# Where the two parts of a split weight lie in SBUF, modulo 256 bytes, in a float32 decoder block on one core

## Chip, core and metric

One NeuronCore of one Trainium2 chip runs the whole program. The metric is the device time of one execution in microseconds (us). The kernel before took 2196.67 us, the median of three runs (2195.61 to 2196.71).

## What is computed

The reference is one layer of a decoder block in float32, on 512 tokens of width 2048:

- RMSNorm, then one input projection. Its columns feed two token mixers: eight heads of dilated sliding-window attention, and eight heads of sparse attention with a compressed, a selected and a window branch mixed by sigmoid gates.
- RMSNorm of each mixer's output, one output projection of width 2048, the residual.
- RMSNorm, then a SwiGLU feed-forward of hidden width 5632: `h + (silu(hn @ w_gate) * (hn @ w_up)) @ w_down`.
- A last RMSNorm.

```
proj = rmsnorm(x) @ w_in
h = x + concat(rmsnorm(o_a), rmsnorm(o_b)) @ w_out
h = h + (silu(hn2 @ w_gate) * (hn2 @ w_up)) @ w_down
```

## The kernel before

**Three products for one.** Every large operand is split in two parts of type float32r: `wh` holds the weight rounded, `wl` the remainder. The activations lie split in the same way in two long-lived tiles `ah` and `al`, and in the feed-forward also in `B11h`/`B11l`, `T1h`/`T1l` and so on. One product is three matmuls into the same bank: `wh` with `ah`, `wh` with `al`, `wl` with `ah` (`mm3`, lines 162 to 165; `mm`, lines 1002 to 1005, is the same without a group check). A 128x128 piece of `wh` or `wl` is the stationary operand, which a weight load (PEld) brings into TensorE; the rows of the activations are the moving operand, 512 or 256 columns long.

**Halves.** Weights come from memory in units of 1024 columns (tile `raw`, four buffers) and, for the down projection, of 512 (`rawd`, two buffers). A `Job` (line 121) turns one half of 512 columns into `wh` (line 134, ScalarE copies and rounds) and `wl` (line 137, VectorE subtracts). `jobs` lists all halves in the order in which TensorE takes them; `next_half` (line 170) hands out one and keeps three or four splits ahead. One half is four stationary pieces, so it feeds 12 matmuls.

**Stages in order.** First the columns for the compressed branch (tiles `pc`), then keys, values and queries with the attention steps woven in (`pp`, and `phid` where the compression weights, units `w1`, are the *moving* operand against the stationary `kvs`), then the output projection (`pab`). These halves come from the loop at line 144; all but `w1` feed matmuls of 512 moving columns. Then 44 blocks `f` of the feed-forward's hidden rows. A block is seven products P1 to P7 of 256 moving columns (a Strassen-Winograd scheme over 2x2 quarters, here "quads"), two halves each, so 168 matmuls; `quad_jobs` (line 743) builds its 14 jobs. In every fourth block from `f` = 4 on, the 16 halves of the down projection for the four blocks before stand between the products (`dn_job`, line 794, and `down`, line 1053; 512 moving columns; banks `pd` and the bank of P3, which the profile groups under the name `P`). The last 16 halves of the down projection go through `kept` (line 797) into room of the activation tiles and are used by `last` (256 columns, `pl`).

**Places.** `placed` (line 82) takes a tile that is 64 elements longer than needed and hands out a slice that begins `at` elements into it. `wsplit` (line 117) chooses `at`: `MH = ML = 32` elements where the job has `even` set, `WH = WL = 16` elements otherwise. The activation tiles use `MH` and `ML`. In the built program all these tiles begin 128 bytes past a multiple of 256, so the activations' rows begin at 0 modulo 256 bytes, weight parts with `even` at 0 too, and weight parts without it at 192, that is 64 bytes below. Each stationary piece is 512 bytes long in a partition and each activation row 2048 or 1024, so every piece of a half keeps its half's place modulo 256. In the kernel before, `even` is set in the first half of P1 of every block (line 788) and nowhere else. Counted in the built program: 4800 matmuls of 512 columns have their `wh` or `wl` at 192; of those of 256 columns in the quads 6864 have it at 192 and 528 at 0.

One other stationary operand has several places: the gate weights `wgs` (lines 266 and 312 to 314) take 192 bytes for each of the 16 steps `k`, so that `k` = 0, 1, 2, 3 lie at 128, 64, 0 and 192 modulo 256, and so on. They are the weights of 512-column matmuls of 48 and of 24 stationary columns.

Of the kernel before, what the change touches and what calls it, by code (L numbers as in the profile page):

```python
# [71 lines left out]
def block_kernel(ctx: ExitStack, tc: tile.TileContext, xt, wst, wdn, smalls, wg, w2c, bias, ident_in, out):  # L72
# [29 lines left out]
    def load_to(n):  # L102
        while state["dma"] < min(n, len(units)):
            u = state["dma"]
            t = wp.tile([128, 1024], F32, tag="raw", name="raw", bufs=LA)
            for k in range(2 if u < TWO else 1):
                c = slice(512 * k, 512 * k + 512) if u < TWO else slice(0, 1024)
                sp.dma_start(t[:, c], wst[u][:, c])
            raws[u] = t
            state["dma"] += 1  # L110

    late = {}
    jobs = []
# [27 lines left out]
    def half_of(u, k):  # L141
        return lambda: raws[u][:, 512 * k:512 * k + 512]

    for u, d in enumerate(units):
        if d[0] != "quad":
            for k in range(2):
                jobs.append(Job(half_of(u, k), load=lambda u=u: load_to(u + 1)))

    n_plain = len(jobs)
    total = n_plain + 14 * FB + KB * NPH  # L150
# [95 lines left out]
    def tokens(*accs):  # L246
        return [[a[:, 128 * t:128 * t + 128] for a in accs] for t in range(accs[0].shape[-1] // 128)]
# [176 lines left out]
    def evac(p, tag, scale=None, keep=False):  # L424

        t = tmp()
        if scale is None:
            dve.tensor_tensor(t, p, r1, op=OP.mult)
        else:
            dve.scalar_tensor_tensor(t, p, scale, r1, op0=OP.mult, op1=OP.mult)  # L430
        ph, pl = (MH, ML) if tag[0] == "k" else (WH, WL)
        h = placed(kvq(tag), S, ph, tag=tag + "h", name=tag + "h")
        l = placed(kvq(tag), S, pl, tag=tag + "l", name=tag + "l")
        act.activation(h, t, AF.Copy)
        dve.tensor_tensor(l, t, h.bitcast(F32), op=OP.subtract)
        return (h, l, t) if keep else (h, l)
# [212 lines left out]
    def proj_block(upto=None):  # L649
        return ps.tile([128, 512], F32, tag="proj", name="pp", bufs=2)  # L650
# [40 lines left out]
    for j in range(NH):  # L691
# [5 lines left out]
        p = proj_block()  # L697
# [8 lines left out]
        p = proj_block()  # L706
# [3 lines left out]
        p = proj_block()  # L710
        for half in range(2):
            in_unit(p, half)
        k = evac(p, "ka")
        v = V()
        queue.append(Att("dil", q, k, v, ba, None, {}, True, True, head_done(j, 0)))
        p = proj_block()
# [10 lines left out]
    dn = {}  # L727
# [9 lines left out]
    def load_fin(n):  # L737
        while len(fin) < min(n, KB // 2):
            k = 2 * len(fin)
            fin.append(wp.tile([128, 1024], F32, tag="raw", name="fin", bufs=LA))  # L740
            sp.dma_start(fin[-1].rearrange("p (n c) -> p n c", n=2), wdn[NPH - 1, k:k + 2].rearrange("n p c -> p n c"))

    def quad_jobs(f, order):

        u = base_u + 4 * f

        def q(i, k):
            return raws[u + i][:, 512 * k:512 * k + 512]

        def comb(o, a, b, op):  # L750
            return lambda: dve.tensor_tensor(o(), a(), b(), op=op)  # L751

        def nxt(i):
            return lambda: load_to(u + 4 + i + 1)

        r = {}
        for k in range(2):
            A11, A21, A22, A12 = (lambda i=i, k=k: q(i, k) for i in range(4))
            if f == 0:
                def s1(A11=A11, A21=A21, A22=A22):  # L760
                    comb(A11, A11, A21, OP.subtract)()
                    comb(A21, A21, A22, OP.add)()

                r["P1", k] = Job(A11, load=nxt(-1))
                r["P5", k] = Job(A21, prep=s1)
                r["P7", k] = Job(A11)
                r["P4", k] = Job(A22)
            else:
                r["P1", k] = Job(A11)
                r["P7", k] = Job(A11, prep=comb(A11, A11, A21, OP.subtract))  # L770
                r["P4", k] = Job(A22, post=comb(A21, A21, A22, OP.add))
                r["P5", k] = Job(A21)
            r["P6", k] = Job(A22, prep=comb(A22, A22, A11, OP.subtract))
            r["P2", k] = Job(A12)
            r["P3", k] = Job(A12, prep=comb(A12, A12, A22, OP.subtract))
        if f + 1 < FB:
            if f == 0:
                r["P6", 1].post = nxt(1)
                r["P3", 1].post = nxt(3)
            else:  # L780
                r["P6", 1].post = nxt(0)
                r["P5", 1].post = nxt(1)
                r["P3", 1].post = nxt(3)
        else:
            r["P6", 1].post = lambda: load_fin(1)
            r["P5", 1].post = lambda: load_fin(2)
            r["P3", 1].post = lambda: load_fin(LA)
        r["P1", 0].even = True
        return [r[p, k] for p in order for k in range(2)]

    ORDER0 = ("P1", "P5", "P2", "P7", "P4", "P6", "P3")
    ORDER = ("P1", "P7", "P4", "P6", "P5", "P2", "P3")

    def dn_job(p, nb):
        return Job(lambda: dn[p, nb], post=load_dn)

    def kept(nb):
        def f():
# [5 lines left out]
    for f in range(FB):  # L804
        qj = quad_jobs(f, ORDER if f else ORDER0)
        p = f // PH - 1
        nb = 0
        for i, name in enumerate(ORDER if f else ORDER0):
            sched.append(("q", f, name))
            jobs += qj[2 * i:2 * i + 2]  # L810
            if f and f % PH == 0 and i:
                for _ in range(3 if i < 5 else 4):
                    if nb < KB:
                        sched.append(("d", p, nb))
                        jobs.append(dn_job(p, nb))
                        nb += 1
    for nb in range(KB):
        jobs.append(Job(lambda nb=nb: fin[nb // 2][:, 512 * (nb % 2):512 * (nb % 2) + 512], dst=kept(nb),
                        post=(lambda nb=nb: load_fin(nb // 2 + LA + 1)) if nb % 2 else None))
# [3 lines left out]
    def out_unit(half, tag="proj"):  # L823
        p = ps.tile([128, 512], F32, tag=tag, name="pab", bufs=2)
        c = 8 - 8 * half
        run_unit([(p, ah[:, c + k, :], al[:, c + k, :], k == 0, k == 7) for k in range(8)])
        return p
# [54 lines left out]
    for nb in range(KB):  # L882
        while "hs" not in rest and (nb == 4 and not idle() or nb == 2 and (queue or cur["s"])):
            step()
        p = out_unit(1, ("proj", "sc", "t")[nb // 2 % 3])
# [86 lines left out]
    for i in range(KB):  # L972
        nb = PASS2[i]
        p = out_unit(0)
# [96 lines left out]
    for kind, a, b in sched:  # L1071
# [3 lines left out]
        f, name = a, b  # L1075
        product(f, name)
        if f == 0:
            if name == "P7":
                r = st["rs2"] = Rsqrt(tokens(sacc), D, rab.v[:, :4])
# [154 lines left out]
```

## Time and profile before

| what | value |
|---|---|
| median of three runs | 2196.67 us |
| the profiled execution's own time | 2196.02 us |
| its span, first to last instruction | 2194.3 us |
| PE busy | 2172.3 us, 13856 matmuls |
| PEld busy | 1951.7 us |
| DVE busy, ACT busy | 1571.1 us, 969.3 us |
| granted TensorE clock, mean | 0.997 |
| HBM read | 223.94 MB |

PE is TensorE's matmul side, PEld its weight loads, DVE is VectorE, ACT ScalarE. "Mean ns of one" of a matmul reaches from its start to the end of its pipeline, and matmuls overlap, so the mean is longer than the distance from one start to the next. That distance, here called the **step**, is read from the start times in the timeline. Times in the timeline count from the span's start.

### The profile page before, as it was taken

Reading aid. Unit: us, or ns where it says so; the run is one execution under the profiler, and the core shown is the slowest. Engines: PE = TensorE matmul, PEld = TensorE weight load, DVE = VectorE, ACT = ScalarE, POOL = GpSimd, SP = SyncE. Lnnn points to the kernel's source line nnn. Section 1 sums busy time; section 2 is a strip of 40 time slices with the busy share of each in tenths; the row PEclk is TensorE's granted clock in tenths of the full one; section 3 lists DMA queues with packets and bytes.
Section 4 is the critical chain, followed back from the end, with each engine's and each line's share of the span. In section 5 each row is a group of like instructions: output and inputs, shape, how many; then the busy total and the mean of one; then the engine's idle time right before and its main releaser. Section 6 shows DMA issues by size and latency. Waiting matters only on the chain.

```text
span 2194.3 us, 35893 instructions
## 1 busy us (share of the span) xinstructions
PE 2172.3 (99%) x13856; PEld 1951.7 (89%) x13856; DVE 1571.1 (72%) x3051; ACT 969.3 (44%) x1861; POOL 39.5 (2%) x46
## 2 busy tenths in 40 slices
PE   9999999999999999999999999999999999999997
PEld 7788888888887888989899999989898999999897
DVE  6755656356667588979687777869596877778686
ACT  6544444344444255535343443435353434434356
POOL 0000000000000000000000000000000000000003
PEclk9999999999999999999999999999999999999999
DMA  6442222322224232333333333333333333333233
GB/s 222 144 137 80 80 80 75 101 79 80 89 75 156 96 96 68 116 115 92 107 111 107 95 113 105 104 95 120 112 97 106 106 111 93 115 106 102 84 124 106
DMA packets 82252, 230.47 MB, mean 105 GB/s; under 512 B 8736, under 2 KB 13216, under 8 KB 82080
## 3 DMA queue, kind: packets, MB, share of 16 engines
q1 hardware_dynamic: 82080, 228.17, 33.3%
q8 instruction: 109, 1.79, 0.3%
q14 instruction: 63, 0.52, 0.1%
HBM read 223.94 MB, written 4.19 MB: 104 GB/s over the span
## 4 chain that ended last, share of the span: by engine, by line
PE 96%; DVE 2%; ACT 1%; issue 0%; DMA 0%; SPq 0%; DVEq 0%; ACTq 0%
PE P L1003 13%; PE P L1005 13%; PE P L1004 13%; PE pp L163 6%; PE pp L165 6%; PE pp L164 6%; PE pd L165 4%; PE pd L164 4%; PE pd L163 4%; PE P L165 3%; PE P L164 3%; PE P L163 3%; PE pab L163 3%; PE pab L165 3%; PE pab L164 3%; PE pt L512 1%
## 5 line engine op out<-in xcount | busy, mean ns | idle before, releaser
L134 ACT ACTIVATE wh<-raw 128x512 fp32r<-128x512 f32 x888 | 548.1, 628 | 524.3 <-PE P L1004 175.3
L137 DVE TENSOR_TENSOR wl<-raw,wh 128x512 fp32r<-128x512 f32 x888 | 596.2, 685 | 65.6 <-ACT wh L134 58.3
L1005 PE MATMUL P<-ah,wl 128*128 128x256 f32 x1056 | 292.3, 277 | 0.2 <-DVE wl L137 0.2
L1003 PE MATMUL P<-ah,wh 128*128 128x256 f32 x1056 | 292.2, 277 | 0.0
L1004 PE MATMUL P<-al,wh 128*128 128x256 f32 x1056 | 292.1, 277 | 0.0
L163 PE MATMUL pp<-ah,wh 128*128 128x512 f32 x640 | 259.1, 405 | 0.0
L165 PE MATMUL pp<-ah,wl 128*128 128x512 f32 x640 | 251.5, 393 | 0.0
L164 PE MATMUL pp<-al,wh 128*128 128x512 f32 x640 | 250.4, 391 | 0.0
L751 DVE TENSOR_TENSOR raw<-raw 128x512 f32<-128x512 f32 x352 | 241.3, 686 | 3.4
L134 ACT ACTIVATE wh<-rawd 128x512 fp32r<-128x512 f32 x160 | 101.1, 632 | 280.6 <-PE pd L164 162.6
L1003 PEld LDWEIGHTS P<-ah,wh 128*128 128x128 f32 x1056 | 199.0, 188 | 0.8
L1004 PEld LDWEIGHTS P<-al,wh 128*128 128x128 f32 x1056 | 198.8, 188 | 0.9
L1005 PEld LDWEIGHTS P<-ah,wl 128*128 128x128 f32 x1056 | 198.8, 188 | 0.5 <-DVE wl L137 0.5
L1067 DVE TENSOR_TENSOR hs<-hs,pd 128x512 f32<-128x512 f32 x98 | 67.3, 687 | 132.5 <-PE pd L165 132.4
L165 PE MATMUL pd<-ah,wl 128*128 128x512 f32 x392 | 154.4, 394 | 0.0
L164 PE MATMUL pd<-al,wh 128*128 128x512 f32 x392 | 153.7, 392 | 0.0
L163 PE MATMUL pd<-ah,wh 128*128 128x512 f32 x392 | 152.1, 388 | 0.0
L165 PEld LDWEIGHTS pp<-ah,wl 128*128 128x128 f32 x640 | 120.2, 188 | 26.4
L164 PEld LDWEIGHTS pp<-al,wh 128*128 128x128 f32 x640 | 120.6, 188 | 19.9
L163 PEld LDWEIGHTS pp<-ah,wh 128*128 128x128 f32 x640 | 120.6, 188 | 19.6
L137 DVE TENSOR_TENSOR wl<-rawd,wh 128x512 fp32r<-128x512 f32 x160 | 109.6, 685 | 22.8 <-ACT wh L134 22.1
L501 ACT ACTIVATE e<-e,st 128x512 f32<-128x512 f32 (+1 forms) x96 | 54.1, 563 | 133.7 <-DVE st L499 133.7
(277 smaller groups left out, 4924.4 us busy)
## 6 DMA issues: line engine op xcount, KB each, us to landing
raw<-in_wst_dram SPq DMA_DIRECT2D x311, 512.0 KB, 3.5
rawd<-in_wdn_dram SPq DMA_DIRECT2D x160, 256.0 KB, 2.6
bias<-in_bias_dram SPq DMA_DIRECT2D x16, 320.0 KB, 2.9
xc<-in_xt_dram SPq DMA_DIRECT2D x16, 256.0 KB, 2.8
hs<-in_xt_dram SPq DMA_DIRECT2D x16, 256.0 KB, 5.3
fin<-in_wdn_dram SPq DMA_DIRECT2D x8, 512.0 KB, 3.7
out_dram<-hs SPq DMA_DIRECT2D x10, 256.0 KB, 2.2
out_dram<-hs SPq DMA_DIRECT2D x3, 512.0 KB, 3.4
```

Of the source, the lines that this page charges most:

```text
L134: act.activation(self.h, self.src(), AF.Copy)
L137: dve.tensor_tensor(self.l, self.src(), self.h.bitcast(F32), op=OP.subtract)
L163: pe.matmul(o, wh, mh, start=start, stop=False)
L164: pe.matmul(o, wh, ml, start=False, stop=False)
L165: pe.matmul(o, wl, mh, start=False, stop=stop)
L501: act.activation(et, et, AF.Exp, bias=m, scale=-1.0, accum_out=den)
L512: pe.transpose(p[:, 128 * (o + b):128 * (o + b) + 128], self.e[t][:, 128 * b:128 * b + 128], ident)
L751: return lambda: dve.tensor_tensor(o(), a(), b(), op=op)
L1003: pe.matmul(o, wh, mh, start=start, stop=False, skip_group_check=True)
L1004: pe.matmul(o, wh, ml, start=False, stop=False, skip_group_check=True)
L1005: pe.matmul(o, wl, mh, start=False, stop=stop, skip_group_check=True)
L1067: dve.tensor_tensor(hs[:, nb, :], hs[:, nb, :], p, op=OP.add)
```

## The change

Three lines of one file. The jobs of all units but the quads get `even`, so do the jobs of the down projection but the last 16, and the first half of P1 keeps it in blocks 0 and 1 alone.

```diff
     for u, d in enumerate(units):
         if d[0] != "quad":
             for k in range(2):
-                jobs.append(Job(half_of(u, k), load=lambda u=u: load_to(u + 1)))
+                jobs.append(Job(half_of(u, k), load=lambda u=u: load_to(u + 1), even=True))
...
-        r["P1", 0].even = True
+        r["P1", 0].even = f < 2
...
     def dn_job(p, nb):
-        return Job(lambda: dn[p, nb], post=load_dn)
+        return Job(lambda: dn[p, nb], post=load_dn, even=True)
```

The instructions, their order on every engine, their sizes and their waits are the same in both programs; addresses differ. Counted in the built program after: the 4800 matmuls of 512 columns have their weight part at 0 modulo 256, the place of the moving rows; 7368 of the quads' matmuls have it at 192 and 24 at 0. In the 128 matmuls of `phid` the moving operand is a weight part, and goes from 192 to 0 against a stationary operand at 128.

## Prediction

> **What bounds the kernel now.** I read the engines' shares first, then the chain that ended last, then the costliest groups.
>
> ```profile
> span 2194.3 us, 35893 instructions
> PE 2172.3 (99%) x13856; PEld 1951.7 (89%) x13856; DVE 1571.1 (72%) x3051; ACT 969.3 (44%) x1861; POOL 39.5 (2%) x46
> PEclk9999999999999999999999999999999999999999
> ...
> PE 96%; DVE 2%; ACT 1%; issue 0%; DMA 0%; SPq 0%; DVEq 0%; ACTq 0%
> ...
> L1005 PE MATMUL P<-ah,wl 128*128 128x256 f32 x1056 | 292.3, 277 | 0.2 <-DVE wl L137 0.2
> L1003 PE MATMUL P<-ah,wh 128*128 128x256 f32 x1056 | 292.2, 277 | 0.0
> ...
> L163 PE MATMUL pp<-ah,wh 128*128 128x512 f32 x640 | 259.1, 405 | 0.0
> ...
> L163 PEld LDWEIGHTS pp<-ah,wh 128*128 128x128 f32 x640 | 120.6, 188 | 19.6
> ```
>
> TensorE is busy 99% of the span at an undiminished clock, and 96% of the chain is matmuls. The groups wait for almost nothing: their last column is 0.0 to 0.2 us. So a change of a matmul's step goes one for one into the time, in both directions: 2194.3 - 2172.3 = 22 us of PE idle time is all that a slower PE could eat into, and it lies where the change hardly reaches (the start, the norm between the two feed-forward parts, the end). ScalarE and VectorE do the same splits as before to other addresses; with 44% and 72% they have room, and a slower PE only gives them more. No DMA, wait or queue moves, so the whole question is what one matmul's step costs when its weight load reads from another place.
>
> **The steps, read from the timeline.** First a run of 36 matmuls of 512 columns in the down projection, weights at 192 modulo 256:
>
> ```profile
> 935.94 0.39 PE L163 MATMUL P<-ah,wh 128*128 128x512 f32 x1
> ...
> 944.18 0.28 PE L1003 MATMUL P<-T4h,wh 128*128 128x256 f32 x1
> ```
>
> (944.18 - 935.94) / 36 = 228.9 ns per step. The means of the same kind in the grouped view show that it isn't the same for the three matmuls of a product:
>
> ```profile
> L165 PE MATMUL pd<-ah,wl 128*128 128x512 f32 x392 | 154.4, 394 | 0.0
> L164 PE MATMUL pd<-al,wh 128*128 128x512 f32 x392 | 153.7, 392 | 0.0
> L163 PE MATMUL pd<-ah,wh 128*128 128x512 f32 x392 | 152.1, 388 | 0.0
> ```
>
> Their mean, 391.3 ns, is 162.4 ns over the step, which is the pipeline behind it; so 388, 392 and 394 are steps of 225.6, 229.6 and 231.6 ns. Now the only place where the trace has weights at the moving rows' own place over a long run: the first half of P1 (12 matmuls of 256 columns, at 0), followed by its second half (12 at 192).
>
> ```profile
> 930.42 0.28 PE L1003 MATMUL P<-B11h,wh 128*128 128x256 f32 x1
> ...
> 931.86 0.28 PE L1003 MATMUL P<-B11h,wh 128*128 128x256 f32 x1
> ...
> 933.22 0.28 PE L1003 MATMUL P<-ah,wh 128*128 128x256 f32 x1
> ```
>
> At 0: 1.44 / 12 = 120.0 ns. At 192: 1.36 / 12 = 113.3 ns. Same operands, same sizes, same engine work beside it: the equal place costs 6.7 ns a matmul at 256 columns.
>
> **The change part by part.**
>
> *Part 1, P1's first half from block 2 on.* 42 blocks go from 120.0 to 113.3 ns for 12 matmuls: 42 x (1.44 - 1.36) = 3.4 us **less**.
>
> *Part 2, the 4800 matmuls of 512 columns* (400 halves of 12: `pc` 16, `pp` 160, `pab` 64, down projection 160). Their step at 0 is not in the trace as a long run. Three kinds of row bound it. The nearest is the gates' product: 512 moving columns at 0, and stationary pieces whose place rotates with `k`. A load runs during the matmul before it. In these rows, the loads for `k` = 10 (at 0) run during the matmuls that start at 56.51 and 56.74, those for `k` = 6 during 54.67 and 54.90; the neighbours load from 64, 128 or 192.
>
> ```profile
> 54.67 0.40 PE L314 MATMUL pg<-al,wgs 128*24 128x512 f32 x1
> 54.90 0.40 PE L313 MATMUL pg<-ah,wgs 128*48 128x512 f32 x1
> 55.14 0.39 PE L314 MATMUL pg<-al,wgs 128*24 128x512 f32 x1
> ...
> 56.06 0.39 PE L314 MATMUL pg<-al,wgs 128*24 128x512 f32 x1
> 56.28 0.39 PE L313 MATMUL pg<-ah,wgs 128*48 128x512 f32 x1
> 56.51 0.40 PE L314 MATMUL pg<-al,wgs 128*24 128x512 f32 x1
> 56.74 0.40 PE L313 MATMUL pg<-ah,wgs 128*48 128x512 f32 x1
> 56.98 0.39 PE L314 MATMUL pg<-al,wgs 128*24 128x512 f32 x1
> 57.21 0.39 PE L313 MATMUL pg<-ah,wgs 128*48 128x512 f32 x1
> 57.43 0.39 PE L314 MATMUL pg<-al,wgs 128*24 128x512 f32 x1
> ```
>
> With the load at 0: 56.98 - 56.51 = 0.47 us for two, and 55.14 - 54.67 = 0.47 for two, 235 ns each. Elsewhere: 56.51 - 56.06 = 0.45 and 57.43 - 56.98 = 0.45, 225 ns each. So a short load costs the long stream some 10 ns when it starts at the stream's place, and nothing visible when it starts elsewhere. The second kind is the change from the output projection to the first P1, where one load at 0 runs under a 512-column matmul:
>
> ```profile
> 843.46 0.39 PE L164 MATMUL pab<-al,wh 128*128 128x512 f32 x1
> 843.68 0.40 PE L165 MATMUL pab<-ah,wl 128*128 128x512 f32 x1
> 843.92 0.28 PE L1003 MATMUL P<-B11h,wh 128*128 128x256 f32 x1
> ```
>
> That matmul (start 843.68) has 0.24 us to the next start, where the three steps worked out above are 225.6 to 231.6 ns. The third is the 256-column pair: the 6.7 ns added to the shortest step, 225.6, gives 232.3. I take **234 ns**, between 232.3 and 235. Ends: 225.6 from below (no step of a long load is shorter, and nothing in the trace shows the stream faster), 240 from above (twice 120.0, as though each 256 columns paid anew). At 234: 4800 x (234 - 228.9) = 24.5 us **more**. From the ends: -15.8 and +53.3 us.
>
> *Part 3, `phid`.* 128 matmuls have the stationary 128 and no longer 192 bytes past the moving place. By the 256-column pair that is at most 128 x 6.7 = 0.9 us in either direction; I take 0.
>
> *Hidden costs.* The splits for these halves read and write the same sizes, and the wait columns above leave them slack; I cost them at nothing. If that cover were gone, a late split would show as a PE wait behind `wl`, which is 0.2 us now in its largest group.
>
> Sum: -3.4 + 24.5 = +21.1 us on the profiled execution's 2196.0 (span 2194.3 and 1.7 around it; 0.6 below the median shown): **2217 us**.
>
> **Rivals.**
>
> *A. The forecast:* the load at the stream's place delays the stream once per matmul. Own range: 232 to 237 ns a step, 2207 to 2232 us. For it: three kinds of row, of 512 columns twice. Against it: none of them is a long run; in the gates' rows and at the border the pattern is disturbed anyway, so a settled run may cost less than its first matmul.
>
> *B. Faster:* the settled run finds the short step. At 192 the 512-column step wanders through 225.6, 229.6 and 231.6, while the 256-column half at 0 settles on a single value. If the collision at 0 delays the load and not the stream, and a 512-column stream has room for a late load (188 ns of load against 226), each step is 225.6: 4800 x -3.3 = -15.8, with part 1 **2177 us**. It decides as soon as the mean step falls below 228.9 + 3.4 / 4.8 = 229.6. Against it: the gates' loads at 0 are short and early, and the stream still loses 10 ns.
>
> *C. Nothing but part 1:* the place matters only where load and stream are about equally long, as at 256 columns, and the longer stream hides it: 2196.0 - 3.4 = **2192.6 us**. The load's 188 ns in the row above fit well under 228.9. By the Trainium skill, page "TensorE: Matmul & The Clock Gate", section "Step-by-step: what each phase is for", TensorE reads moving operand and weights through two independent SBUF ports, so that a load takes no read bandwidth from a running matmul; by that rule both parts would be 0 and the time 2196. The trace disagrees: 120.0 against 113.3 ns in the same product. The rule could still hold where the load isn't what the step waits for; the gates' rows speak against that.
>
> *D. The quads lose their good step.* The 192 place has a second, slower step after a disturbance. In block 0, behind a wait:
>
> ```profile
> 849.87 0.39 PE L1003 MATMUL P<-B21h,wh 128*128 128x256 f32 x1 [0.29 <-ACT ft L1032]
> ...
> 850.33 0.28 PE L1003 MATMUL P<-B21h,wh 128*128 128x256 f32 x1
> ...
> 855.28 0.28 PE L1003 MATMUL P<-ah,wh 128*128 128x256 f32 x1
> ```
>
> 42 matmuls in 4.95 us are 117.9 ns each, and so they stay until P1's first half of block 1, after which they run at 113.3. The change keeps that half at 0 in block 1, but no later one; should the down projection's new places throw the quads out of step, up to 42 x 168 matmuls pay 4.6 ns, 32 us, on top of A: 2250 us. Against it: a run at 0 is just what restores the good step, and no product of the later blocks waits.
>
> *E.* Each 512-column step is 240, the upper end: 2196.0 - 3.4 + 53.3 = 2246 us.
>
> **How the numbers follow.** A 0.62, B 0.20, C 0.08, D 0.06, E 0.04. Predicted is A's 2217 us. The range goes from just under B's 2177, 2176, to A's upper end, 2232, and leaves out D, E and tails. A measurement of this kernel tells about 0.2%, 4.4 us, from no change: faster is B, 0.20; within it is C (4.1 us below the median), 0.08; slower are A, D and E, 0.72.
>
> **What would show it.** Right: the three `pd` rows average some 396 ns where they have 391.3, the `pp` and `pab` rows rise alike, and the `B11` rows of the quads fall to 276. `pd` rows all near 388 show B; unchanged ones C; `P` rows of 256 columns near 280 show D; `pd` near 402 shows E. New idle time in front of matmuls would mean that something besides the place has moved. The weakest step is the 234 ns: it is taken from short runs and from another length of stream.

## The result

The kernel after takes **2219.97 us** (median of five, 2219.71 to 2220.18), before 2196.67 (2195.22 to 2196.71): a ratio of 1.0108, 95% interval 1.0094 to 1.0123. Forecast was 2217 us. The time is right and the reason given for it is wrong: the part that was to cost 24.5 us costs next to nothing, and the part that was to save 3.4 us is where the time went. In three experiments below the times of one kernel fall on two levels at the same granted clock, so there single executions are given in place of a ratio.

The page of the profile after, in the rows that answer to those shown of before:

```profile
span 2218.1 us, 35893 instructions
PE 2195.6 (99%) x13856; PEld 1978.6 (89%) x13856; DVE 1579.4 (71%) x3051; ACT 969.4 (44%) x1861; POOL 39.5 (2%) x46
...
L1005 PE MATMUL P<-ah,wl 128*128 128x256 f32 x1056 | 295.8, 280 | 0.4 <-DVE wl L137 0.4
L1003 PE MATMUL P<-ah,wh 128*128 128x256 f32 x1056 | 294.8, 279 | 0.0
...
L163 PE MATMUL pp<-ah,wh 128*128 128x512 f32 x640 | 260.4, 407 | 0.0
...
L163 PE MATMUL pd<-ah,wh 128*128 128x512 f32 x392 | 152.5, 389 | 0.0
L164 PE MATMUL pd<-al,wh 128*128 128x512 f32 x392 | 152.5, 389 | 0.0
L165 PE MATMUL pd<-ah,wl 128*128 128x512 f32 x392 | 152.4, 389 | 0.0
```

Read them from the bottom. The three `pd` rows, 388, 392 and 394 before, are all 389: the 512-column matmuls of the down projection became *faster*, by 2.0 ns in the mean (391.3 to 389.3). The quads' rows, 277 before, are 279 to 280, though fewer of their matmuls lie at 0. That is the sign which the prediction gave for its rival D.

The border times show where the 23.8 us of the span arise: the first matmul of block 2 and the first of the last stage, in the timeline of before and then of after.

```profile
892.18 0.28 PE L1003 MATMUL P<-B11h,wh 128*128 128x256 f32 x1
...
2134.68 0.28 PE L163 MATMUL pl<-ah 128*128 128x256 f32 x1
```

```profile
844.16 0.28 PE L1003 MATMUL P<-B11h,wh 128*128 128x256 f32 x1
...
890.93 0.28 PE L1003 MATMUL P<-B11h,wh 128*128 128x256 f32 x1
...
2157.54 0.28 PE L163 MATMUL pl<-ah 128*128 128x256 f32 x1
```

| stretch | before | after | difference |
|---|---|---|---|
| up to block 0 | 843.92 | 844.16 | +0.2 |
| blocks 0 and 1 | 48.26 | 46.77 | -1.5 |
| blocks 2 to 43 | 1242.50 | 1266.61 | **+24.1** |
| last stage | 59.62 | 60.56 | +0.9 |

All of it, and a little more, arises in blocks 2 to 43. There the 1920 matmuls of 512 columns give back 1920 x 2.0 = 3.8 us, so the 7056 of the quads cost 27.9 us more, 4.0 ns each.

Now the place where it begins. The timeline after, in block 1:

```profile
877.79 0.28 PE L1003 MATMUL P<-T4h,wh 128*128 128x256 f32 x1
...
879.15 0.28 PE L1003 MATMUL P<-ah,wh 128*128 128x256 f32 x1
...
879.75 0.39 PE L1005 MATMUL P<-ah,wl 128*128 128x256 f32 x1 [0.20 <-DVE wl L137]
...
880.33 0.28 PE L1003 MATMUL P<-ah,wh 128*128 128x256 f32 x1
...
885.28 0.28 PE L1003 MATMUL P<-B21h,wh 128*128 128x256 f32 x1
```

Ahead of the wait 12 matmuls take 1.36 us, 113.3 ns each. A single wait for a split follows (0.20 us of idle time). Behind it 42 matmuls take 4.95 us, 117.9 ns each, with operands of the same kind at the same places and, by the view of stretches, at a granted clock of 1.00 in the whole block; no later half of the quads takes 1.36 us again up to the end. I call the two the **short** and the **slow** step. The profile before has the slow step too, in block 0; there P1's half at 0 in block 1 ends it.

### The profile page after: what moved, and what is told of

It reads as the page before. It is cut to its first block, busy times and chain, and to the rows that moved or that the text cites. A ratio compares the mean times of both kernels' runs of the same rounds, so it can differ in the third digit from the quotient of the medians.

```text
span 2218.1 us, 35893 instructions
## 1 busy us (share of the span) xinstructions
PE 2195.6 (99%) x13856; PEld 1978.6 (89%) x13856; DVE 1579.4 (71%) x3051; ACT 969.4 (44%) x1861; POOL 39.5 (2%) x46
## 4 chain that ended last, share of the span: by engine, by line
PE 96%; DVE 3%; ACT 1%; issue 0%; DMA 0%; SPq 0%; DVEq 0%; ACTq 0%
PE P L1005 13%; PE P L1004 13%; PE P L1003 13%; PE pp L163 6%; PE pp L165 6%; PE pp L164 6%; PE pd L163 4%; PE pd L164 4%; PE pd L165 4%; PE P L163 3%; PE P L164 3%; PE P L165 3%; PE pab L164 2%; PE pab L165 2%; PE pab L163 2%; PE pt L512 1%
## 5 line engine op out<-in xcount | busy, mean ns | idle before, releaser
L163 PE MATMUL pp<-ah,wh 128*128 128x512 f32 x640 | 260.4, 407 | 0.0
L163 PE MATMUL pd<-ah,wh 128*128 128x512 f32 x392 | 152.5, 389 | 0.0
L165 PEld LDWEIGHTS pp<-ah,wl 128*128 128x128 f32 x640 | 120.2, 188 | 27.9
L163 PEld LDWEIGHTS pp<-ah,wh 128*128 128x128 f32 x640 | 120.5, 188 | 19.6
```

Of the source, the lines that this page charges most:

```text
L163: pe.matmul(o, wh, mh, start=start, stop=False)
L165: pe.matmul(o, wl, mh, start=False, stop=stop)
```

## The experiments

The theory after the result, the *wait theory*: the quads at 192 have two steps, a wait throws them into the slow one, a half at 0 brings the short one back, and the change took away all such halves after block 1. Its rivals: the *forecast's theory* (512 columns at 0 cost time after all), and the *neighbour theory* (the 512-column halves at 0 throw the quads into the slow step).

### Both parts apart

The kernel after, with P1's half at 0 in every block again:

```diff
-        r["P1", 0].even = f < 2
+        r["P1", 0].even = True
```

> The kernel after, with P1's first half at place 0 in all 44 blocks, as before the change; the 4800 matmuls of 512 columns stay at 0. Wait theory (the quads' 256-column step is thrown from 113.3 to 117.8 ns by one PE wait in block 1, and a half at 0 brings it back): every block starts in the short step again, the quads cost what they did before, and the 512-column halves keep their gain of about 5 us; about 2190 us, and the 256-column rows of P on the activations at 276 to 277 ns. Forecast's theory (the 512-column halves cost 24 us at 0): 2196.7 + 24 = about 2221 us. Neighbour theory (it is the down projection's halves at 0 that throw the quads out of step): the ten blocks with down projections run at 117.8 from the first such half on, 10 x 150 x 4.5 ns = 7 us more than by the wait theory, about 2197 us.

Measured: **2197.4 us**, ratio to before 1.0006 (0.9996 to 1.0015). So the 4800 matmuls at 0, with all that they do to their neighbours, change nothing that can be measured, and the forecast's theory falls: it asked for 2221. But the wait theory asked for 2190. The timeline shows what is in between, in block 4, before and behind the first run of down projections:

```profile
934.76 0.28 PE L1003 MATMUL P<-ah,wh 128*128 128x256 f32 x1
...
936.12 0.40 PE L163 MATMUL P<-ah,wh 128*128 128x512 f32 x1
...
944.31 0.28 PE L1003 MATMUL P<-T4h,wh 128*128 128x256 f32 x1
...
945.72 0.28 PE L1003 MATMUL P<-T4h,wh 128*128 128x256 f32 x1
...
995.25 0.28 PE L1003 MATMUL P<-B11h,wh 128*128 128x256 f32 x1
...
996.61 0.28 PE L1003 MATMUL P<-ah,wh 128*128 128x256 f32 x1
```

12 quads ahead of it take 1.36 us; the 12 behind it 1.41, with no wait; behind P1's half at 0 of block 5 (to 995.25) it is 1.36 again. The same holds in all ten blocks with down projections: the neighbour theory is true as well. At 120 slow matmuls a block, 10 x 120 x 4.5 ns = 5.4 us, more than the 3.8 us that the down projection's own matmuls gain.

The down projection's halves alone at 0, everything else as before:

```diff
-        return Job(lambda: dn[p, nb], post=load_dn)
+        return Job(lambda: dn[p, nb], post=load_dn, even=True)
```

> The kernel before, with the 160 halves of the down projection alone at 0; the other halves and P1's first half as before. Wait theory, with the step of 226.9 ns read in the profile after: 1920 x (226.9 - 228.9) = -3.8 us, about 2193 us, and the quads' rows unchanged. Forecast's theory: 1920 x 5.1 = +9.8, about 2206 us. Neighbour theory: -3.8 + 7 = about 2200 us, with longer quads in the ten blocks that hold down projections.

Measured: 2197.1 us, ratio 1.0005 (0.9995 to 1.0014), nearer to 2200 than to 2193 or 2206; the ten blocks show the slow step from P4 on, as above. With the 120 slow matmuls a block that were just read, in place of 150, the neighbour theory's price is 2196.2 - 3.8 + 5.4 = 2197.8 us.

The other part alone, P1's half at 0 in blocks 0 and 1 only and all else as before:

```diff
-        r["P1", 0].even = True
+        r["P1", 0].even = f < 2
```

> The kernel before, with P1's first half at 0 in blocks 0 and 1 alone; all 512-column halves stay at 192. The forecast's first part by itself: 42 x 0.08 = -3.4 us, about 2193 us, if the quads keep the short step of 113.3 ns from block 2 on. Wait theory: a PE wait in block 1 behind that half would throw them into 117.8 ns, and no later half at 0 is there to bring them back; then the run of 512-column matmuls at 192 in block 4 or a later one may bring them back, as in the run with no half at 0: single executions near 2193 us and others up to 2222 us, more than one level in the times of one kernel.

Measured: two levels. Of ten executions four took 2190.8 to 2194.1 us and six 2224.4 to 2226.3. The profiled one is of the upper level; its quads after block 1:

```profile
L1004 PE MATMUL P<-al,wh 128*128 128x256 f32 x960 | 268.9, 280 | 0.0
L1003 PE MATMUL P<-ah,wh 128*128 128x256 f32 x960 | 268.0, 279 | 0.0
```

So by itself the term that the prediction set at -3.4 us is about -3 us in some executions and +29 in the others; on top of part 2 it is the whole loss: 2219.97 - 2197.4 = 22.6 us. Only one execution of each two-level kernel was traced. This one has the wait of block 1, 0.20 us, though its program is that of the kernel before up to the end of that block.

### Is it the halves at 0 that keep the short step?

The kernel before with no half at 0:

```diff
-        r["P1", 0].even = True
+        r["P1", 0].even = False
```

> The kernel before, with no half at 0 at all. Wait theory: the waits in block 0 throw the quads into the step of 117.8 ns and nothing brings them back: 44 blocks x 156 x 4.5 ns = +31 us, less 528 x (120.0 - 117.8) = 1 us: about 2226 us. If the short step comes back by itself, or if the half at 0 has nothing to do with it: -528 x 6.7 ns = -3.5 us, about 2193 us.

Measured: two levels again, five executions at 2192.4 to 2194.3 us, five at 2224.0 to 2226.6. The profiled one is of the lower level, and it shows the way out of the slow step without a half at 0, in block 4:

```profile
935.89 0.28 PE L1003 MATMUL P<-ah,wh 128*128 128x256 f32 x1
...
937.31 0.40 PE L163 MATMUL P<-ah,wh 128*128 128x512 f32 x1
...
945.56 0.28 PE L1003 MATMUL P<-T4h,wh 128*128 128x256 f32 x1
...
946.92 0.28 PE L1003 MATMUL P<-T4h,wh 128*128 128x256 f32 x1
```

12 quads take 1.42 us ahead of a run of 36 down-projection matmuls at 192, and 1.36 behind it and from there to the last norm. So a run of 512 columns at 192 can end the slow step, but seldom does: the traces show 76 such runs behind slow quads (50 in part 1 alone, 25 behind the late wait below, 1 here), and this one alone ended it. A run at 0 brings the slow step on.

One half at 0 more in the kernel after, in block 2, behind the wait of block 1:

```diff
-        r["P1", 0].even = f < 2
+        r["P1", 0].even = f < 3
```

> The kernel after, with P1's first half at 0 in blocks 0, 1 and 2, one block more. Wait theory: block 2 brings the short step back, nothing waits behind it until the last norm, and 41 blocks save 12 x 6.7 ns each against the run with that half at 0 in every block: about 2187 us, faster than both kernels. Neighbour theory: short step only until the first down projection in block 4, then 117.8: about 2215 us. Forecast's theory: 2218 us. If a wait comes later than the first half of block 2, the gain is lost and the time is near 2219.

Measured: 2220.9 us, ratio 1.0115 (1.0100 to 1.0130), the quads slow. The expected gain did not come, and the trace shows a third thing: the half at 0 of block 2 ran (12 in 1.44 us), and the half behind it was slow all the same, 12 in 1.41 us:

```profile
893.72 0.28 PE L1003 MATMUL P<-B11h,wh 128*128 128x256 f32 x1
...
895.16 0.28 PE L1003 MATMUL P<-B11h,wh 128*128 128x256 f32 x1
...
896.57 0.28 PE L1003 MATMUL P<-ah,wh 128*128 128x256 f32 x1
```

Block 2 of the first experiment shows the same, and its block 3 then brings the short step back. One half at 0 is thus no sure way: with the other weights at 192, two failed in the traces taken and all others behind slow quads worked.

So the kernel after with eight halves at 0, which can't fail for one bad block:

```diff
-        r["P1", 0].even = f < 2
+        r["P1", 0].even = f < 8
```

> The kernel after, with P1's first half at 0 in blocks 0 to 7. Here the wait in block 1 is followed by six more halves at 0, so it alone can't keep the quads slow. Wait theory alone: short step of 113.3 ns from block 3 at the latest to the end, about 2189 us. Neighbour theory (a run of 512-column matmuls at 0 ends in the slow step, whatever was before): slow from P4 of block 4, short again in blocks 5 to 7, slow from P4 of block 8 to the end, 36 blocks x 168 x 4.5 ns = 27 us over that, about 2215 us.

Measured: 2217.2 us, ratio 1.0100 (1.0083 to 1.0117): the neighbour theory's 2215, not the wait theory's 2189. Block 8 ahead of and behind its down projections, in the timeline (1.36 us for 12, then 1.42):

```profile
1053.69 0.28 PE L1003 MATMUL P<-ah,wh 128*128 128x256 f32 x1
...
1055.05 0.40 PE L163 MATMUL P<-ah,wh 128*128 128x512 f32 x1
...
1063.23 0.28 PE L1003 MATMUL P<-T4h,wh 128*128 128x256 f32 x1
...
1064.65 0.28 PE L1003 MATMUL P<-T4h,wh 128*128 128x256 f32 x1
```

In the kernel after, then, there are two causes in a row, either of which is enough: the wait in block 1, as its trace shows it, and, were that away, the first down projection at 0.

### Does a wait alone do it?

A version without down projections at 0 and with the short step from block 2 on (shown last among the experiments) gets a wait put in late: 30 fills of a constant tile, 165 ns each, on VectorE in block 22, once without and once with halves at 0 behind them.

```diff
+        if f == 22:
+            r["P4", 0].prep = lambda: [dve.memset(ones, 1.0) for _ in range(30)]
```

> The version with pc and the output projection at 0 and P1's first half at 0 in blocks 0 to 7 (2190.3 us), with 30 fills of a constant tile put on VectorE in block 22 ahead of a split (30 x 165 ns = 5 us), so that TensorE has to wait for a split there. The fills write the value that is there already. Wait theory: a wait of a few us or less throws the quads into 117.8 ns, and no half at 0 follows: up to 21 blocks x 168 x 4.5 ns = 16 us more than the wait itself, unless a run of the down projection at 192 brings the short step back earlier: between 2195 and 2211 us, and the rows behind block 22 at 280 in place of 276 for some time. If a wait has no lasting effect: at most 2190.3 + 5 = 2195 us, all rows behind it at 276.

```diff
-        r["P1", 0].even = f < 8
+        r["P1", 0].even = f < 8 or f > 22
```

> The same late fills, and P1's first half at 0 again in blocks 23 to 43. Wait theory: the slow step lasts until the first or second of these halves, then 113.3 again: 2190.3 + the wait (at most 5) + 21 x 0.08 + one or two slow blocks at 0.7 = 2193 to 2199 us in all executions. If the halves at 0 have nothing to do with it: the same as without them plus 1.7 us.

Measured: without, 2213.0 us (nine of ten executions 2212.3 to 2214.6, one 2194.3); with, **2198.1 us** (2197.4 to 2200.0, ten of ten). The wait in the view of waits of the first and of the second (idle us, count, longest; line numbers are two higher there):

```profile
PE P L1007 <- DVE wl L137: 3.2, 2, 3.0
```

```profile
PE P L1007 <- DVE wl L137: 3.4, 3, 3.0
```

The grouped view of the first ahead of block 22 (900 to 1450 us), then of the first behind it (1500 to 2130 us), then of the second in that second stretch:

```profile
L1005 PE MATMUL P<-ah,wh 128*128 128x256 f32 x433 | 119.5, 276 | 0.0
```

```profile
L1005 PE MATMUL P<-ah,wh 128*128 128x256 f32 x496 | 138.4, 279 | 0.0
```

```profile
L1005 PE MATMUL P<-ah,wh 128*128 128x256 f32 x513 | 141.8, 276 | 0.0
```

A wait of 3.2 us makes the kernel 22.7 us slower (2190.3 to 2213.0, some 2 us above the expected range), and a half at 0 in each block behind it takes 15 us of that away. About 5 us of the 22.7 lie in block 22 itself, which takes 24.4 us from its first matmul to the next block's, and 19.0 without the fills. The granted clock drops there too (0.93 over the block), so these two runs alone don't part the wait from the clock; the wait in block 1 of the kernel after came at a clock of 1.00.

The down projection at 192 shows the state as well. Here is the first matmul of its products (L163) in the run without the later halves, in the same two stretches, ahead of the wait and behind it:

```profile
L163 PE MATMUL pd<-ah,wh 128*128 128x512 f32 x177 | 68.7, 388 | 0.0
```

```profile
L163 PE MATMUL pd<-ah,wh 128*128 128x512 f32 x200 | 78.4, 392 | 0.0
```

The three means 388, 392 and 394 are still there behind the wait, but they have moved on by one matmul of the product; in the trace of part 1 alone, L163 is the one with 394. The six traces that have the down projection and the quads' other halves at 192 hold 300 such runs. Where L163 has the shortest of the three steps at the end of a run, the quads behind it have the short step (225 runs); where another has it, they have the slow one (75 runs). So the two states go with the position of a repeating pattern of three matmuls; what sets the position is not shown.

### The two other places, and a half in between

The kernel before with its weight parts at 64, and at 128, in place of 192:

```diff
-MH, ML, WH, WL = 32, 32, 16, 16
+MH, ML, WH, WL = 32, 32, 48, 48
```

> The kernel before, with every weight part that lies at 192 put at 64 modulo 256 (WH and WL 48 elements); P1's first halves stay at 0. A measurement of the step at a third place. If only the load's first row set meeting the stream's first one counts, 64 behaves as 192: 113.3 and 228.9 ns, 2196 us. If the distance counts in the order 0, 64, 128, 192, 64 lies nearer to 0: 256-column steps of 117 to 120 ns, about 2196 + 6864 x 4.5 ns = 2227 us or more, and 512-column steps near 227 ns.

```diff
-MH, ML, WH, WL = 32, 32, 16, 16
+MH, ML, WH, WL = 32, 32, 0, 0
```

> The kernel before, with every weight part that lies at 192 put at 128 modulo 256 (WH and WL 0); P1's first halves stay at 0. A measurement of the fourth place. At 64 the 512-column step was 233.3 ns and the quads' mostly 117.8. If the order of places matters, 128 lies between 64 and 192: 512-column steps of 229 to 233 ns and quads between 113.3 and 117.8, 2197 to 2240 us. If 128 is the place farthest from the stream and so the best, both steps are at or below those of 192 (228.9 and 113.3): 2196 us or less.

Measured: 2239.8 us (1.0199, 1.0178 to 1.0219) and 2248.8 us (1.0242, 1.0221 to 1.0262). One row of the down projection and one of the quads, at 64 and then at 128:

```profile
L1005 PE MATMUL P<-ah,wl 128*128 128x256 f32 x1056 | 296.2, 281 | 0.4 <-DVE wl L137 0.4
...
L165 PE MATMUL pd<-ah,wl 128*128 128x512 f32 x392 | 155.0, 396 | 0.0
```

```profile
L1005 PE MATMUL P<-ah,wl 128*128 128x256 f32 x1056 | 297.8, 282 | 0.1
...
L165 PE MATMUL pd<-ah,wl 128*128 128x512 f32 x392 | 154.8, 395 | 0.0
```

Less 162.4 ns, the 512-column step is about 233 ns at both, against 228.9 at 192 and 226.7 at 0. So for 512 columns the moving rows' own place is the best of the four and the middle ones are the worst. The quads have both steps at 64 as well, but with the roles exchanged: in each of the ten blocks with down projections they take 1.36 us for 12 from P4 on (957.48 to 958.84 us in block 4), and 1.41 behind every half at 0. At 128 their halves take 1.42 to 1.44 us from block 2 on. For 256 columns the short step is thus to be had at 192 and at 64, and at each it can be lost. Neither of the two expectations (a plain order from 0 to 192; only the first meeting counts) fits.

The down projection at 0 except the last half ahead of each group of quads:

```diff
-        return Job(lambda: dn[p, nb], post=load_dn)
+        return Job(lambda: dn[p, nb], post=load_dn, even=nb not in (2, 5, 8, 11, 15))
```

> The kernel before, with the down projection's halves at 0 except the last of each group of three or four, which stays at 192; the rest as before. Neighbour theory in its narrow form (the quads' step is set by the place of the half right before them): the quads in the ten blocks stay at 113.3 ns, and 110 halves x 12 x 2.0 ns are gained: 2196.4 - 2.6 = about 2194 us. If the whole run before the quads counts: slow quads in the ten blocks as with all of them at 0, 2196.4 + 5.4 - 2.6 = about 2199 us. With a half of 12 as a coin toss for the step, in between.

Measured: 2198.1 us, 1.0011 (1.0002 to 1.0021); the quads of the ten blocks are slow as with all halves at 0. Twelve matmuls at 192 do not undo the run ahead of them.

This trace has one thing more. Up to block 4 its program is that of the kernel before, the wait of block 1 is there, and the quads keep the short step behind it, 42 matmuls in 4.76 us:

```profile
879.60 0.38 PE L1005 MATMUL P<-ah,wl 128*128 128x256 f32 x1 [0.19 <-DVE wl L137]
...
880.16 0.28 PE L1003 MATMUL P<-ah,wh 128*128 128x256 f32 x1
...
884.92 0.28 PE L1003 MATMUL P<-B21h,wh 128*128 128x256 f32 x1
```

Ten traces with the weights at 192 have this wait behind quads at the short step, of 0.09 to 0.20 us; in nine the slow step follows, in this one not. So a wait can throw the quads out of step, and mostly does, but it need not.

### A version faster than both

512-column halves at 0 only in `pc` and `pab` (the quads that follow `pab` begin with P1's half at 0), the down projection at 192, and halves at 0 in P1 of blocks 0 to 7:

```diff
-                jobs.append(Job(half_of(u, k), load=lambda u=u: load_to(u + 1)))
+                jobs.append(Job(half_of(u, k), load=lambda u=u: load_to(u + 1), even=d[0] in ("c", "out")))
...
-        r["P1", 0].even = True
+        r["P1", 0].even = f < 8
```

> The kernel before, with the halves of pc and of the output projection (pab) at 0, and P1's first half at 0 in blocks 0 to 7. The attention stage (pp) and the down projection stay at 192. By the two stages' gains in the trace after (pc about -0.7, pab -1.5 us) and 36 x 0.08 = -2.9 us in blocks 8 to 43: 2196.4 - 5.1 = about 2191 us in every execution, because block 5 to 7 bring back the short step after the last wait, and the down projection at 192 keeps it. If the short step doesn't last without a half at 0 in every block: up to 2220 us.

Measured: **2190.3 us** (2189.2 to 2192.2 in eight executions), ratio to before 0.9976 (0.9965 to 0.9986), a small gain but clear of 1. As the late wait shows, it has no protection left behind block 7; halves at 0 in all blocks would cost 36 x 0.08 = 2.9 us of it.

## Why the prediction came out as it did

- **What bounds the kernel**: right. PE is busy 99% of both spans, and every change of a step went into the time.
- **Part 1, "3.4 us less"**: this step failed, and it decided the time. The 6.7 ns a matmul were read rightly, and executions that keep the short step show the gain (2190.8 to 2194.1 for this part alone). But these halves had a second effect that the prediction named and then priced only as part of D: they bring the short step back. So the term is -3.4 us only as long as nothing throws the quads out of step; on top of part 2 it measured +22.6 us (2197.4 to 2219.97).
- **Part 2, "24.5 us more"**: wrong in size and in sign for the matmuls themselves. The long run at 0 has a step of 226.7 ns, in the timeline after:

```profile
938.92 0.39 PE L163 MATMUL pd<-ah,wh 128*128 128x512 f32 x1
...
944.36 0.28 PE L1003 MATMUL P<-T4h,wh 128*128 128x256 f32 x1
```

  That is 24 matmuls in 5.44 us. The prediction took 234 from single matmuls and pairs beside loads of changing place; its own objection, that a settled run may cost less than its first matmul, was the right one. Its nearest source, the gates' product, was also misread. "Nothing visible when it starts elsewhere" does not hold in the rows that it passed over: two matmuls of the trace before, beside which the weights of `k` = 4 load from 128, take the same 0.47 us as those with loads from 0.

```profile
53.74 0.40 PE L314 MATMUL pg<-al,wgs 128*24 128x512 f32 x1
...
54.21 0.39 PE L314 MATMUL pg<-al,wgs 128*24 128x512 f32 x1
```

  Over all steps of that product, the first and those beside a wait left out, it is 235 ns in the mean with a load from 0 and some 229 with any other, so 6 ns and not 10. The gains lie in the down projection (3.8 us), `pab` (1.5) and `pc` (0.5); in `pp`, where attention steps break the runs, the stage takes 2 us more (its L163 row 405 before, 407 after), so that part 2's own sum is about 4 us less. With the quads that it slows behind the down projections the whole part measured about +1 us (2197.4 against 2196.2).
- **Part 3, `phid`**: nothing to be seen by itself: up to block 0 the kernels differ by 0.2 us, the gains and losses of `pc`, `pp` and `pab` included.
- **Rival B** (0.20) described the 512-column step almost exactly (225.6 forecast, 226.7 measured). **Rival D** (0.06) described what the quads did, down to the 117.9 ns and, with part 1, the price (32 - 3.4 = 28.6 us, 27.9 measured in blocks 2 to 43), but as something on top of A. What happened is B's matmuls with D's quads: 28.6 - 15.8 = 12.8 us by their forecast prices, 23.3 measured, mostly since B's -15.8 us was only about -4. D was put aside for two reasons. "A run at 0 is just what restores the good step" holds for P1's halves of 256 columns; the runs of 512 columns at 0 do the opposite. "No product of the later blocks waits" was read from one execution of before. The wait of block 1 is not in that trace, but the change does not make it: the runs with part 1 alone and with the down projection alone have the same program as before up to the end of block 1, and their traces have it, of 0.20 and 0.19 us. A likely reason why that one execution lacks it is its granted clock around the norm in block 0, 0.88, where after had 1.00: a slower TensorE leaves VectorE's splits more time. That is argued, not shown. The two views of stretches (before, then after; the clock is the third figure from the end):

```profile
844.00:873.00 29.00, 26.33 (x193) 25.30 (x192) 25.61 (x64) 14.88 (x32) 0.00 (x0) 0.88 0.23 74
```

```profile
844.20:872.40 28.20, 25.24 (x206) 24.15 (x205) 26.61 (x65) 15.03 (x32) 0.00 (x0) 1.00 0.23 76
```

- **Rival C** (0.08) falls: the 512-column step did move with the place, from 228.9 to 226.7 ns. The rule that stood beside it (the Trainium skill, page "TensorE: Matmul & The Clock Gate", section "Step-by-step: what each phase is for": weights and moving operand have independent read ports, and a load takes no read bandwidth from the running matmul) would leave the time the same at every place. It doesn't agree with these runs: with the same instructions, the place of the weights alone moved the time from 2190.3 to 2248.8 us. Whether a port is shared is not shown by that.
- That 2217 stands so near 2219.97 is chance: a cost of 24.5 us that did not exist, in place of one of 28 that was put aside.

**Open.** Why the quads at 192 have two steps, why a run of 512 columns at 192 now and then ends the slow one and a run at 0 brings it on in each trace, why one wait in ten left the short one alone, and why two halves at 0 out of all failed to bring it back, no run here tells. That `pp` loses at 0 because its runs are broken is argued from its rows, not shown by a run of its own.

## What to carry to other kernels

Where weight loads and moving streams are read at the same time, try the place of one against the other modulo 256 bytes as a size to be tuned, for each length of stream by itself: the best place for one was the worst or the trap for the other. Before an instruction or a layout that looks like waste is removed, ask which state it leaves behind it; the half at 0 cost 0.08 us a block and was worth up to 29 us. A price from a border or from a disturbed stretch is not the price of a settled run; where it must be taken from one, count every row of the kind and not only those that fit. That nothing waits in one trace doesn't say that nothing waits in the next execution. Times of one kernel on two levels are a sign of such a state: look at a trace of each level.

## What the runs showed of the hardware that was not expected

- One stream of 256-column matmuls with the same sizes, places and clock can run at two steps, 113.3 or 117.8 ns, for more than a millisecond, and a wait of 0.20 us can be enough to go from one to the other (a wait of 0.19 us at the same point once was not).
- The step by place of the weights against the moving rows: 512 columns 226.7, 233, 233 and 228.9 ns at 0, 64, 128 and 192; 256 columns 120.0 at 0, 113.3 or 117.8 at 64 and at 192, and 118 to 120 at 128.
- At 192 the three matmuls of a 512-column product differ (225.6, 229.6, 231.6 ns), at 0 they are equal. Which of the three is the shortest goes with the step of the quads that follow.
- No settled run of 512 columns came below 226 ns in the mean. By the formula for an isolated matmul in the Trainium skill, page "TensorE: Matmul & The Clock Gate", section "Back-to-back issue gap", the gap would be 512 / 2.4 + 2.5, an estimate of 215.8 ns; no run here shows it.
